# A two-layer hybrid block on one core: rotary key and dt taken from x in plain float32

## The chip, the core and the metric

The kernel runs on one core of a Trainium2 chip. The metric is the device time of one execution in microseconds (us). Five engines work side by side, each through its own instructions in order: TensorE (PE, with its weight loads listed as PEld), VectorE (DVE), ScalarE (ACT), GpSimd (POOL), and SyncE (SP), which here issues every transfer.

## The reference, cut to what matters

x is 512 tokens by 1024 channels, float32. Two layers follow each other; in each, the parts that the change touches are these:

```
h = rms_norm(x, norm_mix_g[l])                     # x * rsqrt(mean(x*x) + 1e-6) * gain
p = h @ w_in[l]                                    # 1024 -> all branches
k_rope = p[:, 640:672]                             # 32 columns: rotary key, shared by 8 heads
dt     = p[:, last 16 columns of the Mamba part]   # 16 columns, one per head
o_mla  = attention(q, k = [k_nope, rope(k_rope)], v)
o_ssm  = mamba2(..., softplus(dt + dt_bias))
o_rwkv = rwkv7(...)                                # delta-rule state over the tokens
x += (sum of sigmoid(gate_i) * (o_i @ W_br_i)) @ w_out[l]
x += relu(rms_norm(x, norm_ffn_g[l]) @ w_ff1[l])**2 @ w_ff2[l]
```

The norm's factor is one number per token, so the kernel multiplies it in after the product: (x * gain) @ W, then times the factor.

## The kernel before

Activations lie transposed, channels on the 128 partitions and the 512 tokens along the free axis; x is eight tiles of 128x512. A weight block is 1024 input channels by 128 output columns, 128x1024 in memory. Every such block is loaded (`wload`, L239, SP), split into a rounded high part wH and a remainder wL (`split`, L228: ACT casts, DVE subtracts), and so is the operand (hH, hL). A product is then three float32r products per 128 input channels, hH.wH, hL.wH and hH.wL (`mm3`, L259): 24 matmuls of 512 columns per block (`proj`, L268), which the trace names pj, pf, br, wo after their target.

`norm` (L284) makes hH and hL from x, squares x on ACT and adds the squares in two accumulators: acc0 on POOL, acc1 on DVE. `token_sums` (L220) then sums over the channels on PE, in plain float32: for each of four groups of 128 tokens, one matmul with acc0 and one with acc1 as the weights and a single column of ones, in the tile pst. `norm` is called four times: for the mixer and for the feed-forward part of each layer. Ahead of the sums it issues the first two weight blocks (12 and 13 of the RWKV part), behind them one more.

The rotary key and dt are the block `w_krdt`, 1024 by 48. Before, it is one more split product of 24 matmuls in `mla_proj` (L766 and the lines after it); it is the first item of a generator (`mla`, L1202) from which the RWKV stages take one item at a time as filling work for PE. Later four transposes turn the 32 key rows to token-major (krT, L846), and four more the 16 dt rows (dtT, L937).

The order of the work on each engine is not that of the source. The framework sets it when the program is built: it moves whatever is ready in its own reckoning ahead, and each engine then goes through its list strictly in order. Layer 1's `norm` follows directly on the last feed-forward product of layer 0 (pf, L336 to L358), whose last additions to x (L348, DVE) it reads. In layer 0, x comes from memory (`load_x`, L244) while parameters and the first weight block are loaded ahead of it.

Of the kernel before, what the change touches and what calls it, by code (L numbers as in the profile page):

```python
# [8 lines left out]
F32 = mybir.dt.float32  # L9
# [3 lines left out]
ALU = mybir.AluOpType  # L13
# [4 lines left out]
P = 128  # L18
S = 512
D = 1024  # L20
KD = D // P
NC4 = S // P
# [6 lines left out]
B_CQ, B_CKV, B_RW, B_Z, B_XBC, B_G = 0, 3, 5, 19, 27, 39  # L29
# [26 lines left out]
class Kern:  # L56
# [24 lines left out]

    def setup(self):
        nc, c = self.nc, self.const
        self.ident = c.tile([P, P], F32, name="ident")
        make_identity(nc, self.ident)
        self.ones1 = c.tile([P, 1], F32, name="ones1")
        nc.vector.memset(self.ones1, 1.0)
        self.bones = c.tile([P, P], F32, name="bones")
        nc.vector.memset(self.bones, 0.0)
        nc.vector.memset(self.bones[0:64, 0:64], 1.0)  # L90
        nc.vector.memset(self.bones[64:128, 64:128], 1.0)


        self.mst = c.tile([P, 1, 64], F32, name="mst")
        self.msk = c.tile([P, 2, 64], F32, name="msk")
        nc.vector.memset(self.mst, 1.0)
        nc.vector.memset(self.msk, 1.0)
        for hp in range(2):
            h = slice(64 * hp, 64 * hp + 64)
            for d in range(2):  # L100
                p = slice(64 * hp + 32 * d, 64 * hp + 32 * d + 32)
                nc.gpsimd.affine_select(out=self.mst[p, 0, 0:32], in_=self.mst[p, 0, 0:32], pattern=[[1, 32]],
                                        compare_op=ALU.is_gt, fill=0.0, base=0, channel_multiplier=-1)
            nc.vector.memset(self.mst[64 * hp + 32:64 * hp + 64, 0, 32:64], 0.0)
            for t, q, strict in ((self.msk, 1 - hp, True), (self.msk, hp, False)):
                nc.gpsimd.affine_select(out=t[h, q, :], in_=t[h, q, :], pattern=[[1, 64]],
                                        compare_op=ALU.is_gt if strict else ALU.is_ge, fill=0.0, base=0,
                                        channel_multiplier=-1)

        self.mle = c.tile([P, P], F32, name="mle")  # L110
        nc.vector.memset(self.mle, 1.0)
        nc.gpsimd.affine_select(out=self.mle, in_=self.mle, pattern=[[1, P]], compare_op=ALU.is_ge,
                                fill=0.0, base=0, channel_multiplier=-1)
        self.neg = c.tile([P, P], F32, name="neg")
        nc.vector.memset(self.neg, 0.0)
        nc.gpsimd.affine_select(out=self.neg, in_=self.neg, pattern=[[-1, P]], compare_op=ALU.is_ge,
                                fill=-1.0e30, base=0, channel_multiplier=1)

        self.sh = []
        for i in range(2):  # L120
            t = c.tile([P, S + 3], F32, name=f"sh{i}")
            nc.vector.memset(t[:, 0:3], 0.0)
            self.sh.append(t)
        self.shn = 0
        self.pos = c.tile([P, NC4], I32, name="pos")
        self.ones128 = c.tile([P, P], F32, name="ones128")
        nc.vector.memset(self.ones128, 1.0)

    def rope_tables(self):
        nc, c = self.nc, self.const  # L130
# [110 lines left out]
        self.nc.sync.dma_start(out=raw[:, 0:kt * n], in_=self.I["w"][self.l, src] if isinstance(src, int) else src)  # L241
        return self.wsplit(raw, kt, n)

    def load_x(self, pool, src):  # L244
        x, self.xt = [], []
        for k in range(0, KD, 2):
            t = pool.tile([P, 2, S], F32, name=f"x{k}", tag=f"x{k}", bufs=1)
            self.nc.sync.dma_start(out=t, in_=src[k:k + 2].rearrange("k p s -> p k s"))
            self.xt.append(t)
            x += [t[:, 0], t[:, 1]]  # L250
        return x

    def wsplit(self, raw, kt, n):
        H = self.wp.tile([P, 1024], F32R, name="wH", tag="wH", bufs=WB)
# [26 lines left out]

    def norm(self, x, gname, pool, w, ahead):  # L284
        nc = self.nc
        hH = self.hp.tile([P, KD, S], F32R, name="hH", tag="hH", bufs=1)
        hL = self.hp.tile([P, KD, S], F32R, name="hL", tag="hL", bufs=1)
        for k in range(KD):
# [7 lines left out]
        for k in range(KD):  # L296
# [2 lines left out]
            nc.scalar.activation(out=sq, in_=x[k], func=AF.Square)  # L299
            if k >= 2:  # L300
                (nc.vector if i else nc.gpsimd).tensor_tensor(out=acc[i], in0=acc[i], in1=sq, op=ALU.add)
        pst = self.pse.tile([P, S], F32, name="pst", tag="e")
        self.token_sums(pst, acc)
        for b in ahead[2:]:
            first[b] = self.proj(b, ps=self.pse.tile([P, S], F32, name="pj", tag="e"))
        self.rcol = self.rsqrt(self.hp, pst[:, 0:NC4], [P, NC4], 1.0 / D, 1e-6, "n")
# [2 lines left out]
            self.bcast_rows(pb[:, c * P:(c + 1) * P], self.rcol[:, c:c + 1])  # L309
        self.rsb = self.hp.tile([P, S], F32, name="rsb", tag="rsb", bufs=1)  # L310
        nc.scalar.copy(out=self.rsb, in_=pb)
        self.ahead = first

    def scaled(self, out, ps):
# [451 lines left out]
    def mla_proj(self, cp, qp, qT, kvT):  # L766
        nc, l, I = self.nc, self.l, self.I
        PS = lambda name: self.psd.tile([P, S], F32, name=name, tag="d")
        for name, b0, kt, up, nb, n in (("mla_kv_norm_g", B_CKV, 2, "w_ukv", 2, 512), ("mla_q_norm_g", B_CQ, 3, "w_uq", 3, 256)):
            cH, cL = [], []  # L770
            if kt == 2:
                self.krd = qp.tile([48, S], F32, name="krd", tag="krd", bufs=1)
                ps = self.proj(I["w_krdt"][l], 48)
                self.scaled(self.krd, ps[0:48])
                yield
            for j in range(kt):
                ps = self.proj(b0 + j)
                H = cp.tile([P, S], F32R, name="cH", tag=f"cH{j}", bufs=1)
# [49 lines left out]
    def mla_norm(self, pool, pool2, qT, kv):  # L828
# [14 lines left out]
        kr = T("kr", [P, NC4, 1, 32])  # L843
        ps = self.psm.tile([P, S], F32, name="krT", tag="m")
        for c in range(NC4):
            nc.tensor.transpose(out=ps[:, c * 32:c * 32 + 32], in_=self.krd[0:32, c * P:(c + 1) * P], identity=self.ident[0:32, 0:32])  # L846
        nc.scalar.copy(out=kr[:, :, 0, :], in_=ps[:, 0:128].rearrange("p (c d) -> p c d", c=4))
        ksq = T("ksq", [P, NC4, 32])
        nc.scalar.activation(out=ksq, in_=kr[:, :, 0, :], func=AF.Square)
        skr = T("skr", [P, NC4, 1])  # L850
# [81 lines left out]
    def ssm_dt(self, T):  # L932

        nc = self.nc
        ps = self.pss.tile([P, S], F32, name="dtT", tag="r")
        for c in range(NC4):
            nc.tensor.transpose(out=ps[:, 16 * c:16 * c + 16], in_=self.krd[32:48, c * P:(c + 1) * P],  # L937
                                identity=self.ident[32:48, 32:48])
        x, e, u, y, g = (T(n, [P, NC4, 16]) for n in ("dx", "de", "du", "dy", "dg"))
        hb = lambda j: self.hrow[:, j:j + 1, :].to_broadcast([P, NC4, 16])  # L940
        nc.vector.tensor_tensor(out=x, in0=ps[:, 0:64].rearrange("p (c h) -> p c h", c=4), in1=hb(0), op=ALU.add)

        nc.vector.scalar_tensor_tensor(out=u, in0=x, scalar=-1.0, in1=x, op0=ALU.mult, op1=ALU.max)
        nc.scalar.activation(out=e, in_=u, func=AF.Exp, scale=-1.0)
# [214 lines left out]
    def run(self):  # L1159
        tc = self.tc  # L1160
        for l in range(self.depth):
            self.l = l
            first = None
            if l == 0:
                pe_s, self.pse = self.open("pse", space=PSUM, bufs=8 - BK_D)
                xs, xp = self.open("x")
                self.load_params(l)
                first = self.wload(B_RW + 12)
                x = self.load_x(xp, self.I["x"])
                self.nc.sync.dma_start(out=self.pos, in_=self.I["positions"])  # L1170
                self.vfirst = self.dram.tile([4, P, S], F32, name="vfirst")
            self.od = {n: self.dram.tile([k, P, S], F32, name=f"o_{n}{l}") for n, k in (("mla", 4), ("rwkv", 4), ("ssm", 8))}
            self.gd = self.dram.tile([3, 8, P, S], F32, name=f"gd{l}")
            xd = self.dram.tile([8, P, S], F32, name=f"xd_{l}")
            if "mix" not in self.skip:
                ns, npool = self.open("nm")
                self.norm(x, "norm_mix_g", npool, first, [B_RW + j for j in ((12, 13, 8) if l else (12, 13, 4))])
                ns.close()
                for k in range(0, KD, 2):
                    self.nc.sync.dma_start(out=xd[k:k + 2].rearrange("k p s -> p k s"), in_=self.xt[k // 2])  # L1180
# [8 lines left out]
    def mixer(self, xd):  # L1189
# [5 lines left out]
        rwt_s, rwt = self.open("rwt")  # L1195
        mq_s, mqp = self.open("mq", "right")
        mc_s, mcp = self.open("mc", "right")
        self.pad(mqp, 672)
        qT = mqp.tile([P, NC4, 768], F32, name="qT", tag="qT", bufs=1)
        kv = mqp.tile([P, NC4, 8, 160], F32, name="kvT", tag="kvT", bufs=1)  # L1200

# [47 lines left out]
        mg_s, mgp = self.open("mg", "right")  # L1249
        mo_s, mop = self.open("mo", "right")  # L1250
        self.gp = mgp
        self.pad(mgp, 800)
        m = mgp.tile([P, KD, S], F32, name="m", tag="m", bufs=1)

        def rest():
# [114 lines left out]
```

## Time and profile before

| what | value |
|---|---|
| median of three runs | 2142.03 us (2141.42 to 2143.43) |
| the profiled execution | 2140.08 us, of which 2138.1 us span |
| PE busy | 2076.2 us, 97% of the span |
| DVE, ACT, POOL busy | 1343.9, 926.3 and 328.2 us |
| mean granted clock of TensorE | 0.992 |

The span is from the first to the last instruction. A busy PE counts each matmul with its run-out, so matmuls that follow closely overlap: a matmul of 512 columns is listed with 0.39 us and the next begins after 0.23 us. A granted clock of 1.00 is 2.4 GHz, 0.50 is 1.2 GHz.

### The profile page before, as it was taken

Reading aid. Unit: us, or ns where it says so; the run is one execution under the profiler, and the core shown is the slowest. Engines: PE = TensorE matmul, PEld = TensorE weight load, DVE = VectorE, ACT = ScalarE, POOL = GpSimd, SP = SyncE. Lnnn points to the kernel's source line nnn. Section 1 sums busy time; section 2 is a strip of 40 time slices with the busy share of each in tenths; the row PEclk is TensorE's granted clock in tenths of the full one; section 3 lists DMA queues with packets and bytes.
Section 4 is the critical chain, followed back from the end, with each engine's and each line's share of the span. In section 5 each row is a group of like instructions: output and inputs, shape, how many; then the busy total and the mean of one; then the engine's idle time right before and its main releaser. Section 6 shows DMA issues by size and latency. Waiting matters only on the chain.

```text
span 2138.1 us, 30818 instructions
## 1 busy us (share of the span) xinstructions
PE 2076.2 (97%) x12104; PEld 1650.6 (77%) x12104; DVE 1343.9 (63%) x2290; ACT 926.3 (43%) x1594; POOL 328.2 (15%) x240
## 2 busy tenths in 40 slices
PE   8999999999999999999999999999999999999999
PEld 6777777677778888888877777777677788888887
DVE  6886887877666543443557878777775654444434
ACT  5445534664433433333344454356644334333332
POOL 1001020212212111111111011002123111111120
PEclk9999999999999999999999999999999999999999
DMA  5331333124364232322332322322333632222332
GB/s 189 103 110 63 102 114 112 50 86 131 127 223 128 89 101 99 99 97 92 124 119 77 113 74 87 124 82 70 104 133 109 226 123 94 94 99 99 99 97 90
DMA packets 95616, 232.67 MB, mean 109 GB/s; under 512 B 17744, under 2 KB 27088, under 8 KB 95472
## 3 DMA queue, kind: packets, MB, share of 16 engines
q1 hardware_dynamic: 95472, 230.71, 33.1%
q8 instruction: 95, 1.56, 0.3%
q14 instruction: 49, 0.40, 0.1%
HBM read 197.64 MB, written 33.03 MB: 108 GB/s over the span
## 4 chain that ended last, share of the span: by engine, by line
PE 72%; DVE 11%; ACT 4%; issue 3%; DMA 2%; POOL 1%; SPq 0%; DVEq 0%; ACTq 0%; POOLq 0%
PE pj L265 35%; PE pf L265 16%; PE br L265 6%; PE wo L265 4%; DVE wL L232 2%; PE y L1049 2%; PE sc L898 1%; PE up L265 1%; ACT wH L231 1%; PE pT L916 1%; DMA wraw<-in_w 1%; PE YS L647 1%; DMA of<-o_ssm 1%; DVE CW L599 1%; PE o L924 1%
## 5 line engine op out<-in xcount | busy, mean ns | idle before, releaser
L265 PE MATMUL pj<-hH,wH 128*128 128x512 f32 (+1 forms) x1536 | 615.5, 401 | 7.4 <-ACT hH L234 7.4
L265 PE MATMUL pj<-hL,wH 128*128 128x512 f32 (+1 forms) x1536 | 613.0, 399 | 0.2
L265 PE MATMUL pj<-hH,wL 128*128 128x512 f32 (+1 forms) x1536 | 611.5, 398 | 0.9 <-DVE wL L232 0.9
L231 ACT CAST wH<-wraw 128x1024 fp32r<-128x1024 f32 (+1 forms) x314 | 327.4, 1043 | 655.3 <-PE pj L265 288.3
L232 DVE TENSOR_TENSOR wL<-wraw,wH 128x1024 fp32r<-128x1024 f32 (+1 forms) x314 | 415.1, 1322 | 143.2 <-ACT wH L231 142.8
L265 PEld LDWEIGHTS pj<-hH,wH 128*128 128x128 f32 (+1 forms) x1536 | 290.4, 189 | 73.9 <-ACT hH L234 7.4
L265 PEld LDWEIGHTS pj<-hL,wH 128*128 128x128 f32 (+1 forms) x1536 | 290.8, 189 | 65.0 <-issue 4.6
L265 PEld LDWEIGHTS pj<-hH,wL 128*128 128x128 f32 (+1 forms) x1536 | 290.2, 189 | 65.7 <-issue 3.3
L265 PE MATMUL pf<-uH,wH 128*128 128x512 f32 x512 | 199.2, 389 | 0.0
L265 PE MATMUL pf<-uL,wH 128*128 128x512 f32 x512 | 199.2, 389 | 0.0
L265 PE MATMUL pf<-uH,wL 128*128 128x512 f32 x512 | 199.2, 389 | 0.0
L333 POOL TENSOR_TENSOR u<-u,rsb 128x512 f32<-128x512 f32 x64 | 111.5, 1743 | 496.2 <-ACT u L332 474.5
L348 DVE TENSOR_TENSOR x<-x,pf 128x512 f32<-128x512 f32 x128 | 88.1, 688 | 139.0 <-PE pf L265 136.9
L232 DVE TENSOR_TENSOR uL<-u,uH 128x512 fp32r<-128x512 f32 x64 | 44.1, 692 | 138.1 <-ACT uH L231 138.1
L265 PEld LDWEIGHTS pf<-uH,wH 128*128 128x128 f32 x512 | 96.1, 188 | 20.0
L265 PEld LDWEIGHTS pf<-uH,wL 128*128 128x128 f32 x512 | 96.1, 188 | 20.0
L265 PEld LDWEIGHTS pf<-uL,wH 128*128 128x128 f32 x512 | 96.1, 188 | 19.9
L265 PE MATMUL br<-oH,wH 128*128 128x512 f32 x256 | 102.0, 399 | 6.4 <-ACT oH L231 6.4
L265 PE MATMUL br<-oL,wH 128*128 128x512 f32 x256 | 101.9, 398 | 4.3 <-DVE oL L232 4.3
L1036 POOL TENSOR_TENSOR E<-E,CB 128x1280 f32<-128x1280 f32 x16 | 48.7, 3045 | 353.5 <-ACT E L1033 310.7
L265 PE MATMUL br<-oH,wL 128*128 128x512 f32 x256 | 101.1, 395 | 0.0
L335 ACT ACTIVATE u<-u 128x512 f32<-128x512 f32 x64 | 40.5, 633 | 119.1 <-POOL u L333 119.1
(364 smaller groups left out, 2820.9 us busy)
## 6 DMA issues: line engine op xcount, KB each, us to landing
wraw<-in_w SPq DMA_DIRECT2D x302, 512.0 KB, 3.4
gd<-gt SPq DMA_DIRECT2D x48, 256.0 KB, 2.1
th<-gd SPq DMA_DIRECT2D x16, 512.0 KB, 3.9
xd<-x SPq DMA_DIRECT2D x8, 512.0 KB, 5.8
o_ssm<-ys SPq DMA_DIRECT2D x16, 256.0 KB, 2.1
x<-xd SPq DMA_DIRECT2D x8, 512.0 KB, 5.8
of<-o_ssm SPq DMA_DIRECT2D x16, 256.0 KB, 4.3
t<-gd SPq DMA_DIRECT2D x16, 256.0 KB, 2.7
```

The lines of the kernel that those rows point to most:

```text
L231: nc.scalar.copy(out=H, in_=src)
L232: nc.vector.tensor_tensor(out=Lo, in0=src, in1=H.bitcast(F32), op=ALU.subtract)
L265: nc.tensor.matmul(out=ps, lhsT=ww if w_is_lhs else aa, rhs=aa if w_is_lhs else ww, start=first and k == 0 and q == 0, stop=last and k == ...
L333: nc.gpsimd.tensor_tensor(out=u, in0=u, in1=self.rsb, op=ALU.mult)
L335: nc.scalar.activation(out=u2, in_=u, func=AF.Square)
L348: nc.vector.tensor_tensor(out=xk, in0=xk, in1=ps, op=ALU.add)
L599: nc.vector.tensor_tensor(out=CW[o, hp], in0=pv[o], in1=mk, op=ALU.mult)
L647: nc.tensor.matmul(out=pS[m, 256 * hp + i * 64:256 * hp + i * 64 + 64], lhsT=LT[h, hp, i, m], rhs=Z[h, hp, i], start=True, stop=True)
L898: nc.tensor.matmul(out=ps[:, 0:w], lhsT=fT[0][:, j * P:w], rhs=fT[1][:, 0:w], start=True, stop=True)
L916: nc.tensor.transpose(out=ps[:, (j - k) * P:(j - k + 1) * P], in_=Pj[hp][j][:, k * P:(k + 1) * P], identity=self.ident)
L1036: eng.tensor_tensor(out=e, in0=e, in1=CB[g], op=ALU.mult)
L1049: nc.tensor.matmul(out=py[64 * hp:64 * hp + 64, t0:t1], lhsT=X[i][:, k, hp, :], rhs=m, start=k == 0, stop=(d == 0), skip_group_check=True)
```

## The change

- The 48 columns are no longer a split product. `load_wk` loads the 1024x48 block, multiplies the norm's gain into it (DVE, tile wk) and pads each 128-channel group to 64 columns. `norm` then multiplies it with the unsplit x in plain float32: even groups of channels into PSUM partitions 0 to 63, odd ones into 64 to 127 (tile pk). The product stands at the head of `norm` in the source.
- krd becomes a 128x512 tile holding both halves. One plain float32 product with `stk` (two identity blocks on top of each other) adds the halves and turns both key and dt to token-major; dt is kept in a small tile of its own (dtx). `ssm_dt` has no transposes left.
- The two accumulators of squares are added on DVE before the sums over channels, which then take one matmul per group of tokens and not two.
- In layer 0 the transfers stand in another order: parameters, `w_krdt`, the first two tiles of x, the first weight block, the rest of x; x comes in eight transfers and not four.
- Eight plain float32 products of 128x128 ones run at the start of the program, and the constant that they use is the first that DVE makes.
- Two paddings of memory are smaller, so that other tiles keep their places.

```diff
 def setup(self):
+    self.ones128 = c.tile([P, P], F32, name="ones128")
+    nc.vector.memset(self.ones128, 1.0)
     ...
+    self.stk = c.tile([P, 48], F32, name="stk")
+    nc.vector.tensor_tensor(out=self.stk, in0=self.ident[:, 0:48], in1=self.ident[:, 64:112], op=ALU.add)

-def load_x(self, pool, src):
+def load_x(self, pool, src, one=False):
     for k in range(0, KD, 2):
         t = pool.tile([P, 2, S], F32, name=f"x{k}", tag=f"x{k}", bufs=1)
-        self.nc.sync.dma_start(out=t, in_=src[k:k + 2].rearrange("k p s -> p k s"))
+        for d in range(2 if one else 1):
+            a, b = (d, d + 1) if one else (0, 2)
+            self.nc.sync.dma_start(out=t[:, a:b], in_=src[k + a:k + b].rearrange("k p s -> p k s"))
+        if one and k == 0:
+            self.first = self.wload(B_RW + 12)

+def load_wk(self, pool):
+    raw = pool.tile([P, KD, 48], F32, name="wkr", tag="wkr", bufs=1)
+    nc.sync.dma_start(out=raw, in_=self.I["w_krdt"][self.l].rearrange("p (k n) -> p k n", k=KD))
+    wk = pool.tile([P, KD, 64], F32, name="wk", tag="wk", bufs=1)
+    nc.vector.memset(wk[:, :, 48:64], 0.0)
+    g = self.prm[:, COL["norm_mix_g"]:COL["norm_mix_g"] + KD].rearrange("p (k o) -> p k o", o=1)
+    nc.vector.tensor_tensor(out=wk[:, :, 0:48], in0=raw, in1=g.to_broadcast([P, KD, 48]), op=ALU.mult)

 def norm(...):
+    if wk is not None:
+        pk = self.pse.tile([P, S], F32, name="pk", tag="e")
+        for k in range(KD):
+            h = slice(64 * (k % 2), 64 * (k % 2) + 64)
+            nc.tensor.matmul(out=pk[h], lhsT=wk[:, k], rhs=x[k], start=k < 2, stop=k >= KD - 2)
     ...
+    nc.vector.tensor_tensor(out=acc[1], in0=acc[1], in1=acc[0], op=ALU.add)
     pst = self.pse.tile([P, S], F32, name="pst", tag="e")
-    self.token_sums(pst, acc)
+    self.token_sums(pst, acc[1:])
     ...
+    if wk is not None:
+        self.krd = self.hp.tile([P, S], F32, name="krd", tag="krd", bufs=1)
+        self.scaled(self.krd, pk)

 def mla_proj(...):
-            self.krd = qp.tile([48, S], F32, name="krd", tag="krd", bufs=1)
-            ps = self.proj(I["w_krdt"][l], 48)
-            self.scaled(self.krd, ps[0:48])
-            yield
+            self.dtx = qp.tile([P, NC4, 16], F32, name="dtx", tag="dtx", bufs=1)

 def mla_norm(...):
-        nc.tensor.transpose(out=ps[:, c * 32:c * 32 + 32], in_=self.krd[0:32, c * P:(c + 1) * P], ...)
+        nc.tensor.matmul(out=ps[:, c * 48:c * 48 + 48], lhsT=self.krd[:, c * P:(c + 1) * P], rhs=self.stk, ...)
+    nc.scalar.copy(out=self.dtx, in_=pv[:, :, 32:48])

 def ssm_dt(...):
-        nc.tensor.transpose(out=ps[:, 16 * c:16 * c + 16], in_=self.krd[32:48, c * P:(c + 1) * P], ...)
-    nc.vector.tensor_tensor(out=x, in0=ps[:, 0:64].rearrange(...), in1=hb(0), op=ALU.add)
+    nc.vector.tensor_tensor(out=x, in0=self.dtx, in1=hb(0), op=ALU.add)

 def run(self):
+            for _ in range(8):
+                self.nc.tensor.matmul(out=ps[:, 0:P], lhsT=self.ones128, rhs=self.ones128, ...)
```

The first place that moves is the boundary from layer 0's feed-forward part to layer 1's mixer on PE: pf is the last feed-forward product, pj the first weight block of layer 1's mixer. Before:

```order
L265 MATMUL pf<-uH,wH 128x512
L265 MATMUL pf<-uL,wH 128x512
L265 MATMUL pf<-uH,wL 128x512
L265 MATMUL pj<-hH,wH 128x512
L265 MATMUL pj<-hL,wH 128x512
L265 MATMUL pj<-hH,wL 128x512
```

And now, with pk the 48-column product:

```order
L283 MATMUL pf<-uL,wH 128x512
L283 MATMUL pf<-uH,wL 128x512
L309 MATMUL pk<-x_6103,wk 64x512 x2
L309 MATMUL pk<-x_6105,wk 64x512 x2
L309 MATMUL pk<-x_6107,wk 64x512 x2
L309 MATMUL pk<-x_6109,wk 64x512 x2
L283 MATMUL pj<-hH,wH 128x512
L283 MATMUL pj<-hL,wH 128x512
```

All of pk stands between the last pf and the first pj, and needs wk.

The second place is the same boundary on DVE: x is the addition of the last feed-forward product, wL the remainder of a weight block, hL that of the last part of x, acc the squares. Before:

```order
L348 TENSOR_TENSOR x_6117<-x_6117,pf 128x512
L408 MEMSET lw 128x8
L232 TENSOR_TENSOR wL<-wraw,wH 128x1024
L235 SCALAR_TENSOR_TENSOR hL<-x_6117,prm,hH 128x512
L301 TENSOR_TENSOR acc_9213<-acc_9213,sq 128x512 x3
L232 TENSOR_TENSOR wL<-wraw,wH 128x1024
L301 TENSOR_TENSOR acc_9213<-acc_9213,sq 128x512
```

And now:

```order
L376 TENSOR_TENSOR x_6109<-x_6109,pf 128x512
L266 MEMSET wk 128x8x16
L235 TENSOR_TENSOR wL<-wraw,wH 128x1024
L238 SCALAR_TENSOR_TENSOR hL<-x_6109,prm,hH 128x512
L268 TENSOR_TENSOR wk<-wkr,prm 128x8x48
L436 MEMSET lw 128x8
L325 TENSOR_TENSOR acc_9216<-acc_9216,sq 128x512 x4
L326 TENSOR_TENSOR acc_9216<-acc_9216,acc_9215 128x512
```

The multiplication that makes wk stands behind the last addition to x, a wL and an hL.

The third place is the start of the program on DVE, from the middle parts of x to the remainder wL of the second weight block; pf and ang here are the rotary angles. Before:

```order
L235 SCALAR_TENSOR_TENSOR hL<-x_142,prm,hH 128x512 x2
L135 CAST pf<-pos 128x4
L139 TENSOR_SCALAR ang<-pf 128x4 x5
L235 SCALAR_TENSOR_TENSOR hL<-x_144,prm,hH 128x512 x2
L301 TENSOR_TENSOR acc_231<-acc_231,sq 128x512
L139 TENSOR_SCALAR ang<-pf 128x4 x3
L232 TENSOR_TENSOR wL<-wraw,wH 128x1024
```

And now:

```order
L325 TENSOR_TENSOR acc_260<-acc_260,sq 128x512
L238 SCALAR_TENSOR_TENSOR hL<-x_166,prm,hH 128x512 x2
L138 CAST pf<-pos 128x4
L325 TENSOR_TENSOR acc_260<-acc_260,sq 128x512
L142 TENSOR_SCALAR ang<-pf 128x4 x2
L325 TENSOR_TENSOR acc_260<-acc_260,sq 128x512
L142 TENSOR_SCALAR ang<-pf 128x4 x4
L235 TENSOR_TENSOR wL<-wraw,wH 128x1024
```

Three additions of squares stand ahead of that wL and not one, and six angles and not eight.

In the RWKV stages every filling block moves up by one place, since the first is gone. At the end of them in layer 0, between the last state product and the transposes of its output (oT), 67 matmuls of pj stood, and 48 stand now; in layer 1 it was 48 before.

## Rows read from the trace of the kernel before

**Rows 1.** The page, its first part: engine, busy us, share, instructions.

```profile
PE 2076.2 (97%) x12104; PEld 1650.6 (77%) x12104; DVE 1343.9 (63%) x2290; ACT 926.3 (43%) x1594; POOL 328.2 (15%) x240
```

**Rows 2.** PE's waits: line, releaser, us in total, times, longest.

```profile
PE YS L647 <- DVE Z L636: 9.5, 6, 3.4
```

**Rows 3.** The chain that ended last at the layer boundary: start, us, what.

```profile
1071.75 10.88 PE pj L265 x48
1082.63 1.68 PE pst L224 x16
```

**Rows 4.** Timeline of the same boundary: start, us, engine, line, operation.

```profile
1068.93 0.41 SPq L391 DMA_DIRECT2D wa<-in_rwkv_wa  x1
...
1071.59 0.39 PE L265 MATMUL pj<-hH,wH 128*128 128x512 f32 x1
...
1071.79 0.69 DVE L348 TENSOR_TENSOR x<-x,pf 128x512 f32<-128x512 f32 x1 [0.49 <-PE pf L265]
...
1072.70 1.23 DVE L232 TENSOR_TENSOR wL<-wraw,wH 128x1024 fp32r<-128x1024 f32 x1 [0.19 <-ACT wH L231]
...
1073.84 0.75 DVE L235 SCALAR_TENSOR_TENSOR hL<-x,prm,hH 128x512 fp32r<-128x512 f32 x1
```

**Rows 5.** PE groups by form, the 48-column block: count, busy us, mean ns.

```profile
L265 PE MATMUL pj<-hH,wH 128*48 128x512 f32 x16 | 6.4, 399 | 0.0
```

**Rows 6.** Timeline of PE: a plain float32 product of 512 columns, and the next.

```profile
78.46 1.02 PE L525 MATMUL bo<-kk,bones 128*128 128x512 f32 x2
79.32 0.60 PE L533 MATMUL vT<-ident,v 128*128 128x128 f32 x4
```

**Rows 7.** Timeline of PE: plain float32 products in alternating column halves, and the next.

```profile
392.24 2.37 PE L924 MATMUL o<-pT,kvT 128*64 128x512 f32 x16
...
394.54 0.64 PE L888 MATMUL qh<-ident,qT 128*96 128x128 f32 x4
```

**Rows 8.** DVE groups by form: a float32 operation of 256 columns.

```profile
L757 DVE TENSOR_TENSOR o<-o,bo 128x256 f32<-128x256 f32 x16 | 6.7, 419 | 18.8 <-DMA bo<-bod 18.8
```

**Rows 9.** The transfers: bytes and median us from issue to landing.

```profile
wraw<-in_w_krdt SPq DMA_DIRECT2D x2, 192.0 KB, 2.6
```

**Rows 10.** Timeline of layer 1's feed-forward norm.

```profile
1793.00 0.68 DVE L301 TENSOR_TENSOR acc<-acc,sq 128x512 f32<-128x512 f32 x1
...
1794.44 1.84 PE L224 MATMUL pst<-ones,acc 128*128 128x1 f32 x16
```

**Rows 11.** Timeline of the program's start.

```profile
7.37 0.80 PE L265 MATMUL pj<-hH,wH 128*128 128x512 f32 x1 [7.37 <-ACT hH L234]
...
8.86 0.63 PE L265 MATMUL pj<-hH,wL 128*128 128x512 f32 x1
...
9.29 0.63 PE L265 MATMUL pj<-hH,wH 128*128 128x512 f32 x1
...
17.54 1.21 DVE L232 TENSOR_TENSOR wL<-wraw,wH 128x1024 fp32r<-128x1024 f32 x1
...
18.81 0.51 PE L265 MATMUL pj<-hH,wL 128*128 128x512 f32 x1 [0.91 <-DVE wL L232]
...
32.59 0.60 PE L280 MATMUL pb<-ident,ryn 128*128 128x128 f32 x4
```

**Rows 12.** PE by stretches: us, PE busy (instructions), granted clock, DMA share, GB/s.

```profile
21.00:22.00 1.00, 1.00 (x4) 0.50 0.82 262
```

**Rows 13.** The same for stretches with PE idle, and what follows.

```profile
272.00:274.00 2.00, 0.00 (x0) 1.00 0.00 0
...
276.00:278.00 2.00, 2.00 (x6) 0.53 0.16 37
...
1240.00:1242.00 2.00, 0.24 (x2) 1.00 0.65 195
...
1328.00:1330.00 2.00, 0.08 (x1) 1.00 0.00 0
1330.00:1332.00 2.00, 0.97 (x18) 0.71 0.21 78
```

## What was predicted before the run

> **What bounds the kernel now.** I read the page's busy shares first: TensorE is busy for 2076.2 us, 97% of the span [rows 1]. The list of what PE waits for comes next: the longest entry that recurs, the RWKV state products, is 9.5 us in all [rows 2], so apart from the start no stall is large, and what counts is PE's own work and whether the change opens a hole in it. The chain shows that where the change acts in layer 1, PE has no hole at all: 48 matmuls in 10.88 us, the sums over channels right behind [rows 3]. From this comes the unit of the sum: 10.88 / 48 = 0.227 us per matmul of 512 columns at full clock. The times by which the groups of matmuls are listed (399 ns [rows 5]) overlap and are not added.
>
> **The sum, part by part.**
>
> *The split product goes.* 16 matmuls in each of three groups like the one shown [rows 5], so 24 per layer at 0.227 us, 5.44 us. PE is full around them, and no engine waits for krd for long, so I take it whole: -10.9 us for two layers. With the product go a cast on ACT and a subtraction on DVE of 384 columns per layer, off the path; the multiplication that makes wk puts as much back on DVE. The transposes (eight per layer) become eight passes of `stk`, which I set equal: 0.
>
> *The plain product comes.* A plain float32 product is listed as two passes: two of 512 columns stand 79.32 - 78.46 = 0.86 us ahead of what follows [rows 6], 0.43 us each. pk is 8 products, 16 passes, 6.9 us if one follows the other. But they alternate between column halves, and the attention output is the same shape: 16 passes, four each of 512, 384, 256 and 128 columns (as many as ten of 512, 4.3 us), and the next work starts 394.54 - 392.24 = 2.30 us after them [rows 7]. So the halves run side by side and 16 passes of 512 cost 2.30 x 16 / 10 = 3.7 us. The bounds are 3.4 (exactly half) and 6.9. The Trainium skill (TensorEngine Tiling (Array Packing), Tiling Modes) says that tiles work independently but that a change of tiling mode drains TensorE, which would speak against pk between full products. The row agrees on the first, and its 2.30 us already holds a drain at one end; by an extra drain per change the sum would move by some tenths.
>
> *Layer 1: pk waits for wk.* This is the term that decides. On PE pk is the first thing behind the last pf, where pj started at once at 1071.59 [rows 4]. On DVE wk stands behind the last addition to x (1071.79 to 1072.48), a wL (1072.70 to 1073.93) and the last hL (until 1074.59) [rows 4]. Its own 384 columns cost between 0.42 us, the row of 256 [rows 8], and 0.69 us, the addition of 512; I take 0.55. So pk starts at about 1075.1, and PE, with all of pj queued behind pk, stands still for 3.5 us. The transfer of the block is not what is late: it takes the place of the one issued at 1068.93 [rows 4] and lands 2.6 us later [rows 9]. Bounds of the stall: 2 us (if DVE were to run those ahead faster) and 4.5.
>
> *The clock after that stall.* A stretch with 2 us of no matmul at 272 is followed by a granted clock of 0.53 at 276, one at 1328 by 0.71 at 1330; one at 1240 with almost as little work is not (I saw 1.00 in every slice up to 1264) [rows 13]. The slices of half clock in this trace come to some 3.4 us at a time, in which PE loses 1.7 us; I take three in four, 1.3 us, bounds 0 and 1.7. The Trainium skill (TensorE: Matmul & The Clock Gate, Why this matters for your kernels) asks that TensorE not be left idle between bursts of matmuls, or the clock falls back; the rows bear it out in two cases of three, and by it alone the term would be 1.7.
>
> *Sums over channels.* 16 passes take 1.68 us [rows 3], so eight fewer give 0.84 us for each of four norms. The added DVE operation (0.68 us) fits: in layer 1's feed-forward norm the last square is added at 1793.68, and the sums are due at 1794.44 [rows 10]. It is 0.08 us short of being late; I take -0.8 for each of the three norms that are not at the start: -2.4.
>
> *The start, layer 0.* Before, PE began at 7.37, waiting for hH. It ran at half clock (0.43 us from matmul to matmul, 8.86 to 9.29), and then met a wall: the second block's remainder wL, which DVE finished at 18.75 and without which PE sat until 18.81 [rows 11]. Then the clock fell (0.50 at 21 [rows 12]). So what happens ahead of 18.8 is hidden by that wL, the running in on ones, the earlier x and layer 0's pk included, unless wL itself moves. It hardly does: DVE has two more additions of squares ahead of it (2 x 0.68) and some angles fewer. I count on no gain from the early matmuls; on 0.84 for the sums; on half of a fall of the clock avoided (0.5 x 1.7 = 0.85), since pk and the ones leave PE less idle; and on 0.4 lost through the later wL: -1.3, with bounds -3 (no fall, wL earlier) and +1.5 (pk drawn out at half clock, so that the first block itself ends behind wL). The end of this part was the transposes of the norm's factor at 32.59 [rows 11].
>
> *Sum.* -10.9 (split product) + 3.7 (pk, layer 1) + 3.5 (stall) + 1.3 (clock) - 2.4 (sums) - 1.3 (start, with layer 0's pk) = -6.1 us. Layer 1 alone is 3.7 + 3.5 + 1.3 - 0.8 - 5.44 = +2.3 us up to its RWKV stages: there the change loses. The profiled execution took 2140.08 us, its span 2138.1 and 2.0 around it; it lies 1.95 under the median of 2142.03. So 2134.0 for an execution like the profiled one, and 2136 as the median.
>
> **Rivals.**
>
> *The hole in layer 1 does not open, or is hidden.* For it: two of the three operations ahead of wk wait for ACT, and a little less there would bring wk forward; the trace shows slack of 0.2 us, not of 3. Then stall and clock term go, -4.8: 2131. With the start at its best, 2129. Against it: DVE takes its list in order, and the rows give the times.
>
> *The column halves don't run side by side.* pk costs 6.9 us and not 3.7: +3.2 in layer 1, about +1.5 at the start, so -1.4 us, 2140.5. Against it stands the row of the attention output.
>
> *The filling block is missed.* This is the side on which it comes out slower. The RWKV stages take filling blocks one by one, each has moved up by one, and at the end of layer 0's stages 48 matmuls stand where 67 did. If PE idles there for those 19 matmuls, 4.3 us, and the clock falls behind the idle time for another 1.7, and the same holds one step earlier in layer 1, the price is 2 x 6.0 = 12 us: -6.1 + 12 = +5.9, 2148. It decides from 5.2 us per layer on (10.4 us from the forecast to 4.3 over before). With one layer only: 2142. Against it: layer 1 had 48 matmuls in that place before, and PE's list of waits, of which [rows 2] shows the first, names none for these transposes. For it: this is where PE does wait for DVE.
>
> *The falls of the clock are dealt anew.* I counted nine in the slices of the trace, at 1.7 us each, after stalls that the new order shifts; two more or fewer are 3.4 us either way. This is no case of its own but the width of each.
>
> **How the numbers follow.** About 0.2% of the time, 4.3 us, is what can be told from no change here. The forecast (-6.1, its own range 2131 to 2141 with the clock's falls) has a chance of 0.57; the hole hidden 0.18; the halves in series 0.09; the filling block missed in one layer 0.10, in both 0.06. Faster means under 2137.7: most of the hidden hole's (0.17) and three quarters of the forecast's (0.43) make 0.60. Slower means over 2146.3: 0.06 in all. The rest, 0.34, is within. The range is to hold 8 in 10: from 2129.5, the hidden hole with a good start, to 2142.5, the halves in series or one missed block.
>
> **What would show it.** Right: at the layer boundary pk starts some 3.5 us after the last pf, with PE's wait put down to DVE's wk, and a granted clock near 0.5 in the few us behind; pk's 16 passes end within 4 us at full clock; the sums have 8 passes; at the start the third matmul of the second block still waits for wL at 18 to 19.5. Wrong: pk right behind pf, or pk of 7 us; a wait for the output transposes or the state products grown by 4 us; the transposes of the norm's factor before 29 or behind 34 us in layer 0.

## The result and the profile after

The changed kernel takes 2154.29 us (median of five runs, 2153.63 to 2161.06) against 2143.43 us for the kernel before beside it: a ratio of 1.0059, 95% interval 1.0045 to 1.0074. It is slower by some 12 us (10.9 between the medians, 12.6 by the ratio) where 6 us less had been forecast, and the time lies outside the range. The profiled execution of the changed kernel has a span of 2152.6 us against 2138.1, so 14.5 us are to be found.

The page's first line, the one of [rows 1] for the changed kernel:

```profile
PE 2088.9 (97%) x12072; PEld 1657.9 (77%) x12072; DVE 1354.4 (63%) x2297; ACT 925.9 (43%) x1594; POOL 323.4 (15%) x240
```

PE has 32 instructions fewer and is busy 12.7 us longer, so the loss is not idle time in the main. PE's waits after, as [rows 2] (line, releaser, us in total, times, longest):

```profile
PE YS L675 <- DVE Z L664: 7.1, 4, 3.0
...
PE Q L733 <- DVE T L723: 5.4, 2, 3.6
...
PE pk L309 <- DVE lw L436: 3.4, 1, 3.4
```

The stall of pk that the forecast named is there. One entry that it did not name has grown, the wait of the products Q (part of the triangular inverse in the RWKV stages). Before, it stood in two lines, 3.9 us together:

```profile
PE Q L705 <- DVE T L695: 2.2, 1, 2.2
...
PE Q L705 <- DVE rsc L216: 1.7, 1, 1.7
```

The state products YS wait less than before. All idle time of PE together, the span less its busy time, went from 61.9 to 63.7 us only. What grew is the time at half clock. Taken over slices of 1 us, the sum of (1 - granted clock) x busy time is 15.1 us before, in nine falls of 1.4 to 1.7 us each, and 29.2 us after, in nine falls as well: there are not more of them, they last longer.

The next table sets the two profiles against each other between places where the two programs do the same thing. "Moved by" is how much longer the stretch takes after the change, "clock" what the falls of the clock took more, "PE idle" the idle time more, and "rest" what is left, PE's own work; all in us, rounded.

| stretch (before; after) | moved by | clock | PE idle | rest | forecast |
|---|---|---|---|---|---|
| start, to the transposes of the factor (0 to 32.59; 30.88) | -1.7 | -1.7 | -5.9 | +5.9 | -1.3 |
| layer 0, to its last pf (1071.36; 1067.79) | -1.9 | +2.4 | +1.2 | -5.5 | -6.2 |
| boundary, to the transposes of layer 1's factor (1089.75; 1093.96) | +7.8 | +1.5 | +3.4 | +3.0 | +7.7 |
| layer 1, to the end (2138.1; 2152.6) | +10.3 | +11.9 | +3.2 | -4.8 | -6.2 |

In the first row the start's idle time, 9.0 us before and 3.1 after, was filled by the ones and pk, which stand in the rest. The start and the boundary are the forecast within half a microsecond. The miss between these two profiles, 20.6 us, is in the two other rows, 4.3 in layer 0 and 16.5 in layer 1, each behind its norm; 14.3 of it is the clock, 4.4 is idle time, and some 2 are work that the change saved less than forecast.

**The boundary.** Timeline of the changed kernel where [rows 4] stood (start, us, engine, line, operation):

```profile
1068.22 0.69 DVE L376 TENSOR_TENSOR x<-x,pf 128x512 f32<-128x512 f32 x1 [0.49 <-PE pf L283]
...
1069.11 1.23 DVE L235 TENSOR_TENSOR wL<-wraw,wH 128x1024 fp32r<-128x1024 f32 x1
...
1070.26 0.75 DVE L238 SCALAR_TENSOR_TENSOR hL<-x,prm,hH 128x512 fp32r<-128x512 f32 x1
...
1070.93 0.55 DVE L268 TENSOR_TENSOR wk<-wkr,prm 128x384 f32<-128x384 f32 x1
...
1071.53 5.10 PE L309 MATMUL pk<-x,wk 128*64 128x512 f32 x16 [3.35 <-DVE lw L436]
...
1074.75 0.14 PEld L309 LDWEIGHTS pk<-x,wk 128*64 128x64 f32 x2 [0.37 <-issue]
...
1075.18 0.14 PEld L309 LDWEIGHTS pk<-x,wk 128*64 128x64 f32 x2 [0.29 <-issue]
...
1076.57 0.50 PE L283 MATMUL pj<-hH,wH 128*128 128x512 f32 x1
```

The order on DVE is the one that was read off: the last addition to x, a wL, the last hL, then wk in 0.55 us. PE stands for 3.35 us (3.5 forecast; the view names the instruction behind wk on DVE, a short memset). The weight loads show the pairs of pk 0.43 us apart at full clock, so two column halves do run in the time of one: eight pairs, 3.44 us. The first ones ran at half clock, 5.04 us in all up to pj.

**The start.** Timeline, as [rows 11]:

```profile
10.46 0.39 PE L283 MATMUL pj<-hL,wH 128*128 128x512 f32 x1
10.69 0.40 PE L283 MATMUL pj<-hH,wL 128*128 128x512 f32 x1
...
19.38 0.50 PE L283 MATMUL pj<-hH,wL 128*128 128x512 f32 x1 [0.61 <-DVE wL L235]
...
30.88 0.60 PE L298 MATMUL pb<-ident,ryn 128*128 128x128 f32 x4
```

The matmuls of the first block are 0.23 us apart and not 0.43, so in this execution the work ahead of them, the ones and the first half of pk, did raise the clock. It brings little, as forecast: PE waits until 19.4 for the same wL of the second block. The 1.7 us of the table's first row are the fall that the kernel before has there [rows 12]. It is a matter of the execution: in the profiles of runs 4 and 11 below, whose start is the old one, there is no such fall, and the transposes stand at 30.87 and 31.01 us.

**The clock.** Stretches of PE as in [rows 12] (us, PE busy (instructions), granted clock, DMA share, GB/s). Before, around the inverse of layer 0 and of layer 1:

```profile
172.00:176.00 4.00, 3.32 (x69) 0.72 0.31 98
176.00:180.00 4.00, 4.00 (x135) 0.86 0.02 4
180.00:184.00 4.00, 4.00 (x103) 1.00 0.02 4
...
1248.00:1252.00 4.00, 3.09 (x129) 1.00 0.20 70
1252.00:1256.00 4.00, 3.31 (x145) 1.00 0.36 129
```

And after:

```profile
168.00:172.00 4.00, 2.31 (x66) 0.75 0.01 4
172.00:176.00 4.00, 4.00 (x124) 0.50 0.23 65
176.00:180.00 4.00, 4.00 (x80) 0.50 0.18 71
180.00:184.00 4.00, 4.00 (x78) 0.55 0.02 4
184.00:188.00 4.00, 4.00 (x22) 1.00 0.00 0
...
1240.00:1244.00 4.00, 1.87 (x9) 0.72 0.42 131
1244.00:1248.00 4.00, 4.00 (x13) 0.50 0.00 0
...
1260.00:1264.00 4.00, 2.35 (x70) 0.78 0.00 0
1264.00:1268.00 4.00, 4.00 (x138) 0.50 0.02 4
1268.00:1272.00 4.00, 4.00 (x38) 0.50 0.02 4
```

A fall costs 1.4 to 1.7 us where it lasts shortest, 3.4 us at half clock. After the change the falls at 170 and 1262 last four and three times as long (6.8 and 5.1 us lost), those at 272, 1139, 1242 and 1344 twice (2.6 to 3.4 us lost). The two longest stand at the triangular inverse, in layer 0 and in layer 1. What PE does there shows in the timeline of layer 0. Before:

```profile
172.68 1.23 PE L705 MATMUL Q<-T,NA 32*32 32x32 f32 x64 [2.23 <-DVE T L695]
173.84 0.80 PE L265 MATMUL pj<-hH,wH 128*128 128x512 f32 x1
...
176.27 0.26 PE L714 MATMUL X<-NA,Q 32*32 32x32 f32 x1
```

And after:

```profile
169.69 1.75 PE L733 MATMUL Q<-T,NA 32*32 32x32 f32 x64 [3.58 <-DVE T L723]
171.37 0.80 PE L283 MATMUL pj<-hL,wH 128*128 128x512 f32 x1
171.97 0.63 PE L283 MATMUL pj<-hH,wL 128*128 128x512 f32 x1
172.52 0.69 PE L619 MATMUL A<-AR,BK 64*64 64x128 f32 x4
```

PE has come to the inverse earlier, waits 3.58 us for DVE and not 2.23, and has two products of 512 columns left between Q and X, the inverse's next products, and not five. Then come hundreds of products of 32 to 128 columns, and all that time the clock stays at 0.50, until 183.6 us. In layer 1 the wait ahead of Q is about the same (1.78 us after, 1.72 before), and again two wide products are left of five. Nothing near this place was touched: it is the filling blocks, moved up by one, that are elsewhere.

### The profile page after: what moved, and what is told of

Same layout as the page of the kernel before. It is cut to its first block, busy times and chain, and to the rows that moved or that the text cites. A ratio compares the mean times of both kernels' runs of the same rounds, so it can differ in the third digit from the quotient of the medians.

```text
span 2152.6 us, 30771 instructions
## 1 busy us (share of the span) xinstructions
PE 2088.9 (97%) x12072; PEld 1657.9 (77%) x12072; DVE 1354.4 (63%) x2297; ACT 925.9 (43%) x1594; POOL 323.4 (15%) x240
## 5 line engine op out<-in xcount | busy, mean ns | idle before, releaser
L283 PE MATMUL pj<-hH,wH 128*128 128x512 f32 x1520 | 608.1, 400 | 1.3 <-DVE sh L343 0.7
L283 PE MATMUL pj<-hH,wL 128*128 128x512 f32 x1520 | 603.3, 397 | 0.8 <-DVE wL L235 0.8
L283 PE MATMUL pj<-hL,wH 128*128 128x512 f32 x1520 | 602.6, 396 | 0.0
L283 PEld LDWEIGHTS pj<-hH,wH 128*128 128x128 f32 x1520 | 287.7, 189 | 70.2 <-issue 5.7
L283 PEld LDWEIGHTS pj<-hL,wH 128*128 128x128 f32 x1520 | 287.7, 189 | 62.9 <-issue 5.0
L283 PEld LDWEIGHTS pj<-hH,wL 128*128 128x128 f32 x1520 | 287.7, 189 | 62.8 <-issue 2.2
```

Source lines behind the costliest of these rows:

```text
L283: nc.tensor.matmul(out=ps, lhsT=ww if w_is_lhs else aa, rhs=aa if w_is_lhs else ww, start=first and k == 0 and q == 0, stop=last and k == ...
```

## The experiments

Two theories. **O**: the order of the filling blocks, moved up by one because the 48-column block is no longer among them, sets how long PE stands still in the RWKV stages and what it has to do behind a stall; so the clock falls longer. **P**: the falls come as chance has it, and any shift in time deals them anew. Times are medians; the ratio is to the kernel before on the same chip.

**1. The blocks back in their stages.** One number per layer in the table that says how many blocks each preparation stage takes:

```
-PF = ((0, 0, 1, 1), (1, 1, 1, 1))
+PF = ((0, 0, 0, 1), (0, 1, 1, 1))
```

> The changed kernel, with one filling block fewer taken in the RWKV preparation of each layer, so that every later filling block stands in the stage in which it stood before the change. Theory O (the order of the filling blocks sets where PE stalls and what follows a stall, and so how long the clock stays at half): the falls of the clock cost about 15 to 17 us as before and not 29, so 2154.3 - 12.6 = about 2142 us (2139 to 2145), mean granted clock 0.991 or more. Rival P (any shift in time deals the falls anew, the order has no part in it): within 3.4 us of 2154, clock 0.985 to 0.988.

2141.21 us, ratio 1.0009 (0.9995 to 1.0024). The mean granted clock over its eleven executions is 0.9895, in the five of the changed kernel 0.984. The order is worth 13 us by the medians, 11 by the ratios; P, as the account of the slowdown, is out. But the order is not the whole miss. The changed kernel with its blocks in place is 1 us below to 5 us above the kernel before, where the sum, which held no price for the order, said 6 below. The lower clock (0.9895 against 0.991 for the kernel before) makes about 3 us of that; the remainder is not taken apart here.

**2. pk behind the two weight blocks** (the loop over pk moved in `norm`, behind the first two `proj`):

> The changed kernel, with pk behind the two weight blocks of the norm and not ahead of them (at the start pk is moved in the same way). Theory: the stall of 3.35 us at the layer boundary goes, and with it the clock fall of 1.47 us behind it; the falls in layer 1's RWKV stages stay, since the filling order there is the same: 2154.3 - 4.8 = 2149.5 us (2147 to 2152). Rival P (the falls depend on when a stall comes, not on the order): with everything in layer 1 about 5 us earlier they are dealt anew, anything from 2142 to 2158. Rival S (the stall was cover for the sums over channels that follow): the wait moves to the sums, 2154.

2151.87 us, ratio 1.0046 (1.0033 to 1.0059), 2.4 us under the changed kernel's median, at a clock of 0.985. The intervals of the two ratios overlap, so this run alone does not show a gain; run 3 against run 1, the same edit, does. The stall at the boundary is gone from the profile. At the start, where pk moved as well, PE waited for the first block's cast, and the transposes of the factor came at 34.4 us and not at 30.9; run 9 asks whether that counts.

**3. Both edits:**

> Both edits on the changed kernel: filling blocks kept in their stages, pk behind the two weight blocks. Theory O: 2142 - 4.8 = 2137 us (2134 to 2140), below the kernel before. Rival P: 2149 or no rule at all.

2135.84 us, ratio 0.9978 (0.9968 to 0.9987): faster than before. The price of the order shows again, 16 us between runs 2 and 3, and pk's place is worth 5.4 us by the medians of runs 1 and 3, where 4.8 had been expected.

**4. The kernel before, with the blocks moved up**, and not a product more or less:

```
                 ps = self.proj(I["w_krdt"][l], 48)
                 self.scaled(self.krd, ps[0:48])
-                yield
```

> The kernel before, with one edit: the 48-column block and the block after it are one filling item and not two, so that all later filling blocks move up by one, as in the changed kernel, while the work is the same to the last product. Theory O: the falls of the clock grow as in the changed kernel, 2143.4 + 10 = about 2153 us (2149 to 2158), clock 0.986 to 0.988. Rival P: no change beyond 3 us, 2143 (2140 to 2147), clock 0.992.

2155.01 us, ratio 1.0068 (1.0053 to 1.0083). The order alone, with the same work, makes as large a slowdown as the whole change. Its stretches around the inverse of layer 0:

```profile
172.00:176.00 4.00, 1.76 (x66) 0.96 0.01 4
176.00:180.00 4.00, 4.00 (x133) 0.50 0.13 32
180.00:184.00 4.00, 4.00 (x81) 0.50 0.28 103
184.00:188.00 4.00, 4.00 (x68) 0.50 0.02 4
188.00:192.00 4.00, 4.00 (x14) 0.50 0.01 2
```

All of PE's idle time in it is 62.2 us, as before (61.9), while the clock took 26.0 us and not 15.1: of the 11.6 us by which its span is longer, 10.9 are the clock. The profiled execution is the fastest of six. Over all six the mean clock is 0.986 against 0.991, which is some 11 us of the 14; the other 3 are not located.

**5. Layer 1 alone kept in its stages** (run 3 with `PF = ((0, 0, 1, 1), (0, 1, 1, 1))`):

> The kernel of the third run with the filling blocks of layer 0 moved up again, those of layer 1 kept in their stages. Theory O, with most of the price in layer 1 (in the profile of the changed kernel 11.9 of the 14.1 us that the clock lost more lie in layer 1): 2135.8 + 4 = 2140 us (2137 to 2143). Rival: both layers cost the same, half of the 16 us between the second and the third run: 2144. Rival: all of it is layer 1's: 2136.

2143.08 us, ratio 1.0008 (0.9997 to 1.0020). My expectation missed by a little, and the rival of equal shares lies nearer: layer 0's order is worth 7.2 us and layer 1's 8.8 by the medians, about the same. The single profile of the changed kernel, in which layer 0 lost only 2.4 us more, was no measure of the mean.

**6. One block more ahead of Q** (run 3 with `FILL = [0, 1, 1, 1, 2, 1, 1]`):

> The kernel of the third run with one filling block more taken ahead of the products Q of the triangular inverse (L733 in the changed kernel), where PE stands idle for 2.2 us in layer 0, and all blocks behind it moved up by one. Theory I (what costs is the stall ahead of the inverse's small products: while they run, the clock stays at half): the stall goes, the 5 us lost to the clock in layer 0's inverse go, 2135.8 - 2.2 - 4 = about 2130 us (2127 to 2133). Rival M (moving blocks up costs wherever it begins, by stalls in the state products behind): as the second run, 2148 to 2152.

2141.53 us, ratio 1.0001 (0.9988 to 1.0013): between the two, so both readings missed. The stall in layer 0 shrank from 2.2 to 1.8 us only. The loss at the inverse of layer 0 is gone from the profile and the mean clock is as in run 3 (0.991), yet the time is 5.7 us longer.

**7. The start undone** (run 3 without the ones, with the loads in the old order):

> The kernel of the third run without the eight products of ones, and with x and the first weights loaded in the order before (x in four transfers, the block of 48 columns behind x). Theory: what lies ahead of the remainder wL of the second block is hidden by it, so that products and transfers are worth half a fall of the clock at most: 2135.8 + 0.9 (2135 to 2138). Rival: the changed start is worth the 1.7 us by which the transposes of the norm's factor came earlier, and a whole fall besides: 2139.

2134.55 us, ratio 0.9975 (0.9960 to 0.9990): no difference from run 3. Between the old start and the new one with pk late there is nothing to choose.

**8. The kernel before with the summed accumulators alone:**

> The kernel before with the summed accumulators alone. Forecast's term: eight passes fewer, 0.84 us, in three or four norms: 2140.7 - 2.4 to 3.4 = 2138 us. Rival: the added DVE operation makes the sums wait, no change, 2141.

2136.43 us, ratio 0.9978 (0.9963 to 0.9992): 4.5 us less, with the forecast term of 2.4 to 3.4 inside the interval. The added operation on DVE is hidden: in the profile PE never waits ahead of these sums.

**9. Blocks kept, pk early in layer 0 and late in layer 1:**

> The changed kernel with the filling blocks kept in their stages in both layers, and pk behind the two weight blocks in layer 1 alone; in layer 0 pk stays ahead. In the third run the transposes of layer 0's norm factor came at 35.43 us, in the changed kernel at 30.88: 2135.8 - 4.5 = about 2131 us (2128 to 2135). Rival: what is won at the start is given back by a fall of the clock later, 2135.

2136.39 us with 2143.0 for before on this chip, ratio 0.9971 (0.9956 to 0.9986). The gain over run 3 cannot be told from nothing, and the expected 4.5 us did not come: the rival's figure did. An earlier end of layer 0's start is not shown to be worth anything.

**10. Run 9 without the ones:**

> The kernel of the ninth run without the eight products of ones at the start. Forecast (the remainder wL of the second block ends the start in any case): the same within 1.5 us. Rival (without them pk and the first block run at half clock and the first block ends behind wL): 2 to 5 us slower, the transposes of the norm's factor behind 32.5 us.

2136.02 us, ratio 0.9965 (0.9952 to 0.9978). The same, as forecast. The transposes of the factor come 0.8 us later than in the changed kernel and 0.7 earlier than in run 9 (32.35):

```profile
31.64 0.60 PE L298 MATMUL pb<-ident,ryn 128*128 128x128 f32 x4
```

**11. The kernel before, shifted by 1.7 us of work in layer 1's norm:**

> The kernel before with two plain float32 products of 512 columns (0.86 us each) added in layer 1's norm ahead of the transposes of its factor; no other instruction moves on PE. Rival P (falls of the clock depend on the moment at which a stall comes, any shift deals them anew): more than 3 us either way beside the 1.7 us of work. Theory O (the order of the work sets them): 1.7 us slower, 0.5 to 3.

2142.05 us, ratio 0.9994 (0.9982 to 1.0006), so between 3.9 us less and 1.3 more. One shift, in layer 1, without a new order brings nothing like the 12 us; that even the 1.7 do not show is not explained.

**12. The wait ahead of Q filled with products** in the changed kernel:

```
+            if g == 0:
+                for _ in range(5):
+                    nc.tensor.matmul(out=ps, lhsT=self.ident, rhs=Xf[:, 0:512], start=True, stop=True)
```

> The changed kernel with five plain float32 products of 512 columns (identity by the inverse's matrix X, result not used) ahead of the inverse's products Q, in each layer. They can start when X is done, some 4 us before Q (165.64 to 169.67 in the profile of the changed kernel), and stand in the wait for the transposes of X; the blocks ahead are otherwise taken as in the changed kernel, but the last 1.6 us of them come behind Q. Theory I (the clock falls because PE idles ahead of the inverse, and stays down while only its small products run): the 6.8 and 5.1 us lost there to the clock go for the most part, 2154.3 - 8 = about 2146 us (2142 to 2149), at about 8 us more products. Rival: the stall isn't what makes the clock fall there, the products cost what they cover or more: 2154 to 2158.

2150.57 us, ratio 1.0046 (1.0031 to 1.0062). The mean clock of its eight executions is 0.991, as in the kernel before, against 0.984 in the changed kernel. Its profile at both inverses:

```profile
168.00:172.00 4.00, 4.00 (x7) 0.58 0.00 0
172.00:176.00 4.00, 3.91 (x116) 1.00 0.41 135
176.00:180.00 4.00, 3.68 (x121) 1.00 0.02 4
...
1260.00:1264.00 4.00, 3.90 (x202) 1.00 0.01 4
1264.00:1268.00 4.00, 4.00 (x110) 1.00 0.01 4
```

In layer 0 the fall still begins, behind 2.35 us in which PE waits for X, but it ends during the wide products, and the small ones behind run at full clock. So here the small products did not bring the clock down. The time that was to follow, 2146 us, did not come: the added passes take what the clock gives back, and Q itself comes later:

```profile
167.42 6.23 PE L732 MATMUL Q<-X,ident 128*128 128x512 f32 x10 [2.35 <-DVE X L717]
173.58 1.20 PE L736 MATMUL Q<-T,NA 32*32 32x32 f32 x64
```

Q begins at 173.58, against 169.69 without the ten passes. Against the profile of the changed kernel the clock takes 9.7 us less (19.5), PE idles 4.0 us less, and its own work is 10 us more.

**13. The same in the kernel of run 10,** with four products:

> The kernel of the tenth run with four such products ahead of Q in each layer. Theory I: in layer 0 the 2.2 us of idle time ahead of Q are covered and the clock's loss there (5.1 us in the profile of the tenth run, 1.7 in that of the ninth) goes: 0.9965 becomes 0.995, some 3 us less than the tenth run's 2136. Rival: the products cost as much as they save, 2136 to 2138.

2141.38 us with 2138.2 for before, ratio 1.0013 (0.9999 to 1.0028): a loss of 10 us in ratio to run 10. Both readings missed. The clock (0.991) had little left to win, and the products cost more than they cover.

**14. The block of run 6 in layer 0 alone,** on the kernel of run 10:

> The kernel of the tenth run with one filling block more ahead of the inverse's products Q in layer 0 alone. In the profiles of the third and the sixth run layer 0 from the transposes of its norm factor to the feed-forward sums took 696.5 and 690.6 us, layer 1 the same way 701.9 and 711.9: the edit gains 6 us in layer 0 and loses 10 in layer 1. Theory: in layer 0 alone it gains 6, a ratio of 0.9965 - 0.0028 = 0.9937 (0.992 to 0.996). Rival (the two profiles differ by chance of the clock's falls): the same ratio as the tenth run, 0.9965.

**15. Run 10 again beside it:**

> The kernel of the tenth run once more, on the chip of the run beside it: 0.9965 as before (0.9952 to 0.9978).

2138.08 us, ratio 0.9970 (0.9955 to 0.9986), and 2134.85 us, ratio 0.9960 (0.9943 to 0.9978). No gain: the 6 us that two single profiles differed by in layer 0 were not there in the mean. Why run 6 is slower than run 3 stays open.

**All profiles together** show what the order does and what it leaves to chance. For the inverse of layer 0, with one figure per profile in the last column, the runs 6, 12, 13 and 14 left out, which change this very place:

| order in layer 0 | PE waits ahead of Q | 512-column products left between Q and X | clock at 0.50 there, us |
|---|---|---|---|
| as before: the kernel before, runs 1, 3, 7, 8, 9, 10, 11, 15 | 2.2 us | 5 | 3.4, 10.2, 10.2, 3.4, 10.2, 3.4, 10.2, 0, 0 |
| moved up: the changed kernel, runs 2, 4, 5 | 3.4 to 3.6 us | 2 | 13.7, 20.5, 17.1, 20.5 |

In layer 1 the changed kernel and run 2 have 10.2 and 20.5 us there and run 4 none. None of the ten profiles with the old order in layer 1 (the nine of the first row, and run 5) has a fall there; run 14, whose layer 1 is in the old order too, has one of 6.8 us that begins near the inverse's end. In all seventeen profiles every stretch of more than 6.8 us at half clock lies at one of the two inverses; elsewhere it is 3.4 or 6.8. So chance has a large part in one execution, from nothing to 10.2 us with the same order, and the order shifts what chance deals from. That it is the small products behind Q that keep the clock down is what the timelines and run 12 suggest; in layer 0 the longer wait changes with them, and no run takes the two apart there.

The kernel of run 10 (blocks kept in their stages, pk ahead in layer 0 and behind the first two blocks in layer 1, no ones) is the best: 0.9965 and 0.9960 of the time before, some 8 us less.

## Why the prediction was wrong, point by point

All that the prediction named as signs of being right at the boundary, in the sums and at the start came, and none of its signs of being wrong; the loss came where it looked for no sign.

- **The split product, -10.9.** Nearly borne out: in layer 0 what is left besides clock and idle time is -5.5, against 5.44 for the 24 products and 0.8 for the sums; in layer 1 it is -4.8 of the same 6.2.
- **pk, 3.7 in layer 1.** 3.44 at full clock; the halves run side by side. The rival that they don't is out. The drain at a change of tiling that the Trainium skill names (TensorEngine Tiling (Array Packing), Tiling Modes) is no visible term: 16 passes took 5.04 us up to the next pj, and 3.44 at full clock with the 1.47 that the half clock cost leave 0.13 us for it.
- **The stall, 3.5, and the fall behind it, 1.3.** 3.35 and 1.47. The rival in which the hole does not open is out.
- **Sums, -0.8 a norm.** In layer 1 the way from the sums to the transposes shrank from 7.28 to 6.38 us; run 8 agrees.
- **The start, -1.3.** -1.7 between the two profiles, with wL of the second block still the end. The agreement is luck: the 1.7 is one fall in the execution of the kernel before, and with the old start runs 4 and 11 reach the transposes as early (30.87 and 31.01 us against 30.88). Right, and for the reason given, that the ones are worth nothing (run 10).
- **The step that failed** is the one on the RWKV stages. The prediction saw that each filling block had moved up by one, and priced it in one place alone, the end of the state chain ("48 matmuls stand where 67 did"), as idle time, with a chance of 0.16 for one layer or both; slower by more than 4.3 us had 0.06. Neither output transposes nor state products wait longer after the change; the state products even wait less, 7.1 us and not 9.5. And it set the falls of the clock aside: "no case of its own but the width of each", 1.7 us a fall, two more or fewer. In its place runs 1 and 4 showed that moving the blocks costs 11 to 14 us, the same size as that rival's 12 by luck, for it comes another way: mostly by the clock (10.9 of the 11.6 us in run 4's profile), with the same idle time and as many falls. The long falls stand at the triangular inverse, to which PE comes with less left to do: in layer 0 it waits longer for DVE, in both layers little but small products follows. There the half clock lasted three to six times 3.4 us. The price of 1.7 us a fall was read off a profile in which every fall was short; what follows a stall was not read.
- What is left open: with the blocks back in place (run 1) the changed kernel is still some 8 us above the sum. About 1 is the start and about 3 the clock; the remainder is open, and the interval of run 1 is itself 6 us wide.
- The rule that TensorE should not be left idle between bursts of matmuls, or the clock falls back (the Trainium skill, TensorE: Matmul & The Clock Gate, Why this matters for your kernels), is borne out by most of the stalls of 2.2 to 3.6 us here, though not by all: in the kernel before PE stood for 2.42 us at 1240, and the clock stayed at 1.00. By run 4 the larger part of the price is how long the clock then stays down.

## What to carry to other kernels

When a piece of filling work goes, every later piece moves up into a stage for which it was not meant; look at each stall that the schedule was tuned around, not only at the last one, and give the later pieces their stages back first. When a fall of the clock is priced, read what the engine does after the stall: here every fall of more than 6.8 us stood where hundreds of small products follow, and a price read off short falls was several times too low. And the order of an engine that stands first in the list (here DVE ahead of wk) tells a new wait to a few tenths of a microsecond.

## What the runs showed of the hardware that was not expected

One and the same program spreads widely: 35 executions of the kernel before, beside runs 5 to 8, took 2130.56 to 2149.92 us, with mean granted clocks from 0.987 to 0.996. The long ones are in the main those with the lower clock. Three runs, with which this study began, lay within 2 us and told nothing of that; differences of 5 us needed ten executions and more.

While PE ran small products (32 to 128 columns), a clock of 0.50 stayed for some 12 us (the changed kernel, 172 to 184; 20.5 us in runs 2 and 5, with wide products at the end), though the engine was listed as fully busy. Away from the inverses each fall lasted 3.4 or 6.8 us; the one at 1139 in the changed kernel took 6.8 with little but 512-column products in it. The same small products did not bring down a clock of 1.00, neither behind wide ones (run 12, 172 to 180) nor in layer 1 of the kernel before (1248 to 1256).
